# A two-layer hybrid trunk: POOL's elementwise work in the mixers and qkv moves to DVE, and half of the S5 state copies from DVE to ACT

## The chip, the cores and the metric

The kernel runs on one core of a Trainium2 chip. The metric is device time in microseconds (us), and lower is better. A core has five engines with a queue of instructions each: PE (matmul; the weight loads are listed as PEld), DVE (VectorE), ACT (ScalarE), POOL (GpSimd) and SP (SyncE, which here only starts transfers). Each works through its own queue in order, and semaphores make one engine wait for another. POOL can start transfers too.

## The reference

The model is one inference step of a two-layer trunk with D = 1024 on 1280 tokens: 1024 latent and 256 context tokens. Layer 0 feeds one input projection to two mixers. One is a bidirectional S5, a diagonal complex recurrence of 32 groups with 16 channels and 64 states each, then a GLU; the other a bidirectional gated linear attention (GLA) with 4 heads in chunks of 64 tokens. Layer 1 is grouped-query attention with rotary positions. A squared-ReLU MLP of width 4096 follows each.

```python
lam_bar = jnp.exp(lam * dt)
b_bar = ((lam_bar - 1.0) / lam)[..., None] * Bm
bu = jnp.einsum('blgc,gpc->blgp', uc, b_bar)
...
_, hs = lax.associative_scan(_lin_rec, (a, bu), reverse=rev, axis=1)
...
y = y + jnp.real(jnp.einsum('blgp,gcp->blgc', hs, Cm))
...
g = jax.nn.gelu(y.reshape(B, L, S5_WIDTH))
out = g * jax.nn.sigmoid(g @ w_glu.astype(f32) + b_glu.astype(f32))
```

A chunk of the GLA multiplies queries and keys by exponentials of a running sum of gates, and carries a state S from chunk to chunk:

```python
b = jnp.cumsum(gc, axis=1)
qd = qc * jnp.exp(b)
kd = kc * jnp.exp(-b)
...
S = S * jnp.exp(b_last)[..., None] + jnp.einsum('bshk,bshv->bhkv', kc * jnp.exp(b_last[:, None] - b), vc)
```

## The kernel before

**Numbers.** All is fp32. A matmul gets fp32 accuracy from a split: a high part `hi`, which ACT rounds by a copy, and a low part `lo = src - hi`, an elementwise subtraction. `dense` (L404 to L406) is three matmuls per 128 rows: hi·hi, lo·hi, hi·lo. Weights come by `wload`: a transfer on SP's queue, ACT's copy (L236), and the subtraction (L237), on POOL unless an engine is given, into a ring of four tiles. `split` (L384, L385) and `affine` (L391 to L393) do the same for activations. Tokens go in three blocks of 512, 512 and 256.

**Layer 0.** After the adaLN sums and the first norm come the projections of the S5 input u; then side jobs run between the matmuls of the projections of q, k, v and r. A side job is a Python generator; `dense` gives it a turn each time some modelled microseconds have passed (`tick`), and a tile scheduler with a model of the engines then sets the order of every queue.

- `s5_prep` and `s5_tables` build the tables of the S5: complex products with `cmul` (L417 to L422, six elementwise instructions) and two halves of 24 triples of products, three instructions on DVE (L652 to L654) and three on POOL (L656 to L658), sixteen times over.
- `s5_in` runs over 16 pairs of groups. For each, `cmul` makes weights, on POOL for every third pair and on DVE else; PE transposes them (L719) and multiplies (L755). For direction 0 ACT copies the states from PSUM to SBUF (L758), for direction 1 DVE does (L760); a small DVE copy per direction (L761) keeps the final states. After every four pairs `s5_join` combines neighbours: three products (L790) and six sums (L795) on DVE for each of two directions.
- `s5_chain` is 38 serial steps, each a multiply (L813) and two sums (L817, L818) on DVE. Then come eight joins, by four units and two directions; the last of them runs on POOL.
- `gla_gates` makes twelve tiles of gates: a matmul (L1000), ACT's exponentials, DVE's minimum (L1003), scan (L1009, L1011), difference (L1017) and product (L1020), and on POOL a subtraction (L1006) and two products (L1021, L1022). Results go to memory by SP's queue and come back as `wkd`.
- `s5_out` loads its tables kd, cld and ug on POOL's queue (L855, L857, L858), multiplies, and applies the GELU; `glu` projects the result. `gla_first` transposes the returned keys (L1067), multiplies (L1078) and forms 76 chunk states on DVE (L1091). `gla_second` uses them, with one product on POOL (L1196).

**Layer 1.** In qkv, `rope_tile` shuffles on DVE (L1736), multiplies on POOL (L1737) and on DVE (L1738) and sums on DVE (L1739), 20 times with 512 elements; the weights of q are subtracted on POOL. The MLPs' and the attention's own work on POOL (L1463, L1902, L1999, L2000) is another matter and stays.

Of the kernel before, what the change touches and what calls it, by code (L numbers as in the profile page):

```python
# [5 lines left out]
F32 = mybir.dt.float32  # L6
# [4 lines left out]
OP = mybir.AluOpType  # L11
# [213 lines left out]

def wload(s, src, n=1024, eng=None, own=False):

    nc = s.nc
    hi, lo = [s.A([n], F32R) for _ in range(2)] if own else (s.wr[0](), s.wr[1]())
    st = s.A.f32(lo)  # L230
    shp = list(src.shape)
    dst = st[:, :n]
    if len(shp) == 3:
        dst = dst.rearrange("p (a b) -> p a b", a=shp[1])
    nc.sync.dma_start(dst, src)
    nc.scalar.activation(hi[:, :n], st[:, :n], AF.Copy)  # L236
    (eng or nc.gpsimd).tensor_tensor(lo[:, :n], st[:, :n], hi[:, :n].bitcast(F32), OP.subtract)  # L237
    return hi, lo
# [142 lines left out]
def split(s, hi, lo, src, k=0):  # L381

    nc = s.nc
    nc.scalar.activation(hi, src, AF.Copy)  # L384
    (nc.gpsimd if k % 2 else nc.vector).tensor_tensor(lo, src, hi.bitcast(F32), OP.subtract)  # L385


def affine(s, t, a, b, hi, lo, k):

    nc = s.nc  # L390
    nc.scalar.activation(hi, t, AF.Identity, bias=b, scale=a)  # L391
    nc.vector.tensor_scalar(t, t, a, b, OP.mult, OP.add)
    (nc.vector if k % 4 == 0 else nc.gpsimd).tensor_tensor(lo, t, hi.bitcast(F32), OP.subtract)  # L393

# [137 lines left out]
def s5_prep(s):  # L532
# [62 lines left out]
    for d in range(2):  # L595
        cfb = [cf[:, i, 16 * d:16 * d + 16, None].to_broadcast([128, 16, 16]) for i in range(2)]
        cmul(nc.gpsimd, Bb[:, 0, 16 * d:16 * d + 16], Bb[:, 1, 16 * d:16 * d + 16], cfb,
             [t.B[:, 0], t.B[:, 1]], w1, w2)
# [38 lines left out]
def s5_tables(s):  # L637
# [6 lines left out]
    for st in range(8):  # L644
        un, b = divmod(st, 2)
        CL = cl()
        for d in range(2):
# [6 lines left out]
            e.tensor_tensor(CL[:, 0, d], CL[:, 0, d], tw[0], OP.subtract)  # L654
            e = nc.gpsimd
            e.tensor_tensor(CL[:, 1, d], P[0], C[2], OP.mult)  # L656
# [37 lines left out]
def s5_in(s):  # L694
# [12 lines left out]
    def weights(g2):  # L707
        wt, t1, t2 = wtr(), tr[0](), tr[1]()
        a = [pin[:, j, :, g2, :, None].to_broadcast(sh) for j in range(2)]
        b = [Bb[:, j, :, g2, None, :].to_broadcast(sh) for j in range(2)]  # L710
        cmul(nc.gpsimd if g2 % 3 == 0 else nc.vector, wt[:, 0], wt[:, 1], a, b, t1, t2)
        return wt
# [27 lines left out]
    for g2 in range(16):  # L740
# [9 lines left out]
        for d in range(2):  # L750
# [6 lines left out]
            if d == 0:  # L757
                nc.scalar.activation(H[0][:, g2, :, 1:160], pv[:, :, 0:159], AF.Copy)  # L758
            else:
                nc.vector.tensor_copy(H[1][:, g2, :, 0:159], pv[:, :, 1:160])  # L760
            nc.vector.tensor_copy(fin[:, :, d, g2], pv[:, :, 160 + d])  # L761
# [36 lines left out]
def s5_chain(s):  # L798
# [30 lines left out]
    for un in range(4):  # L829
        for d in range(2):  # L830
            e, t = (nc.gpsimd, tm2) if (un, d) == (3, 1) else (v, tmp)
            s5_join(s, e, t, un, d, 4, 2, 0, 40)
            s5_join(s, e, t, un, d, 2, 1, 0, 80)
            yield 2.0
# [144 lines left out]
def gla_gates(s):  # L979
# [7 lines left out]
    for hp in range(2):  # L987
        for tb, (t0, n, _) in enumerate(TBS):
# [7 lines left out]
            for d in range(2):  # L996
# [8 lines left out]
                nc.scalar.activation(a, a, AF.Ln, bias=1.0)  # L1005
                nc.gpsimd.tensor_tensor(mm, mm, a, OP.subtract)  # L1006
                b, r, w = a, s.rst[:, :n], mm
# [12 lines left out]
                v.scalar_tensor_tensor(e, e, 0.125, q, OP.mult, OP.mult)  # L1020
                nc.gpsimd.tensor_tensor(f, f, k, OP.mult)  # L1021
                nc.gpsimd.tensor_tensor(w, w, k, OP.mult)  # L1022
                for h in range(2):
# [77 lines left out]
def gla_second(s, hm):  # L1101
# [63 lines left out]
    def finish(u):  # L1165
# [21 lines left out]
        for h in range(2):  # L1187
# [7 lines left out]
            v.scalar_tensor_tensor(os[h][:, :n], os[h][:, :n], s.gla_norm, pb[:, :n], OP.mult, OP.mult)  # L1195
            nc.gpsimd.tensor_tensor(os[h][:, :n], os[h][:, :n], rt[:, h, :n], OP.mult)  # L1196
            split(s, *acts(hm[tb])(4 + 2 * hp + h), os[h][:, :n])
# [183 lines left out]
def mixer_half(s, l, w_src, h):  # L1381

    nc = s.nc
    wsrc = w_src.rearrange("(k p) m -> p k m", p=128)
    for j in range(4):
        w = wload(s, wsrc[:, 0:4, 256 * j:256 * j + 256], eng=nc.vector)
        for tb in range(3):
# [5 lines left out]
def mixer_out(s, l, w_src, key, part, h, ready):  # L1393
# [10 lines left out]
    if l == 0:  # L1404
        kept = [wload(s, wsrc[:, 4:8, 256 * j:256 * j + 256], eng=nc.vector, own=True) for j in range(4)]

    def weights(m):
        if l == 0:
            w = kept[m // 2]
            return lambda tb: dense(s, w, 4, lambda k: acts(h[tb])(4 + k), TBS[tb][1], off=128 * (m % 2), ms=256)  # L1410
        w = wload(s, wsrc[:, :, 128 * m:128 * m + 128], eng=nc.vector)
        return lambda tb: dense(s, w, KT, acts(h[tb]), TBS[tb][1])
# [319 lines left out]
def rope_tile(s, out, x, t0, n):  # L1732
# [3 lines left out]
    nc.vector.stream_shuffle(sw[:, :n], x, [i ^ 1 for i in range(32)])  # L1736
    nc.gpsimd.tensor_tensor(out, x, s.rope[0][:, t0:t0 + n], OP.mult)  # L1737
    nc.vector.tensor_tensor(sw[:, :n], sw[:, :n], s.rope[1][:, t0:t0 + n], OP.mult)  # L1738
# [18 lines left out]
def qkv(s, h):  # L1757
# [100 lines left out]
    for gi, grp in enumerate((tiles[0:4],) + tuple(tiles[i:i + 1] for i in range(4, 12))):  # L1858
        ws = [wload(s, wsrc[:, :, 128 * c:128 * c + 128], eng=nc.vector if gi == 0 else None) for _, _, c in grp]
        for tb in range(3):  # L1860
# [507 lines left out]
```

## Time and profile before

| | before |
|---|---|
| median of 3 runs | 3299.71 us (3296.11 to 3301.27) |
| profiled execution, its own time | 3298.78 us |
| its span, first to last instruction | 3296.4 us |
| mean granted TensorE clock, share of full speed | 0.960 |
| PE busy | 3063.6 us (93%) |
| PEld busy | 2563.4 us (78%) |
| DVE busy | 2259.9 us (69%), 4290 instructions |
| ACT busy | 1333.8 us (40%) |
| POOL busy | 726.1 us (22%), 659 instructions |

The profile is of one execution. An engine is busy while an instruction of its own runs; time in which it waits counts as idle, but an instruction that has begun and is held up within is listed with a longer duration. Over the whole span the shares say little, since layer 0's mixers make up only the first fifth; stretches say more. The groups below are single lines of such views.

### The profile page before, as it was taken

What the parts mean: (1) busy time and instruction counts of PE and PEld (TensorE: products, weight loads), DVE (VectorE), ACT (ScalarE), POOL (GpSimd) and SP (SyncE); (2) the same over time, 40 slices, a digit from 0 to 9 for tenths busy, and PEclk for the clock granted to TensorE, in tenths of its full rate; (3) what the DMA queues carried; (4) which work ended last, traced back from release to release, by engine and by line L of the source; (5) the groups of instructions that cost most, each with busy time, mean ns of one, the idle gap of its engine ahead of it and who ended that gap; (6) DMA issues with size and microseconds to landing.
All of it is one profiled execution on the core that took longest, in us unless ns stands there. A gap on an engine that the chain in (4) does not pass through costs nothing. (4 is left out here: it accounts for less than half of the span.)

```text
span 3296.4 us, 48459 instructions
## 1 busy us (share of the span) xinstructions
PE 3063.6 (93%) x17458; PEld 2563.4 (78%) x17458; DVE 2259.9 (69%) x4290; ACT 1333.8 (40%) x2485; POOL 726.1 (22%) x659
## 2 busy tenths in 40 slices
PE   7987876999999999999987999999999999999999
PEld 3665556887888887777776888888988888888787
DVE  4576993557876575767875467777488665677868
ACT  3321422423533353423332257777354333543332
POOL 3443452010000013333402212211000000244332
PEclk9998887999999999999988989999999999999999
DMA  9532668533443465656421100100435334543424
GB/s 324 145 91 84 188 204 246 186 114 104 141 138 131 138 202 192 202 166 201 134 80 50 66 31 20 33 14 16 147 122 175 133 123 138 168 141 97 134 92 155
DMA packets 402083, 433.89 MB, mean 132 GB/s; under 512 B 45708, under 2 KB 286820, under 8 KB 396212
## 3 DMA queue, kind: packets, MB, share of 16 engines
q1 hardware_dynamic: 398704, 418.66, 39.8%
q0 software_dynamic: 3136, 12.13, 1.2%
q8 instruction: 138, 2.26, 0.3%
q14 instruction: 105, 0.83, 0.1%
HBM read 296.78 MB, written 133.92 MB: 131 GB/s over the span
## 5 line engine op out<-in xcount | busy, mean ns | idle before, releaser
L1453 PE MATMUL banks<-sb_512r 128*128 128x512 f32 x5376 | 1280.3, 394 | 35.8 <-DVE sb L1649 24.0
L1453 PEld LDWEIGHTS banks<-sb_512r 128*128 128x128 f32 x5376 | 1001.5, 190 | 264.5 <-issue 29.8
L1462 ACT ACTIVATE sb_512r<-sb 128x512 fp32r<-128x512 f32 x786 | 482.8, 630 | 851.9 <-DMA sb<-in_w_mlp_out 212.8
L1463 POOL TENSOR_TENSOR sb_512r<-sb,sb_512r 128x512 fp32r<-128x512 f32 x256 | 350.6, 1396 | 1450.2 <-DMA md<-sb 949.4
L1463 DVE TENSOR_TENSOR sb_512r<-sb,sb_512r 128x512 fp32r<-128x512 f32 x530 | 400.4, 787 | 52.1 <-ACT sb_512r L1462 47.4
L1649 DVE TENSOR_TENSOR sb<-sb,banks 128x512 f32<-128x512 f32 x472 | 319.0, 683 | 158.2 <-PE banks L1453 145.5
L404 PE MATMUL banks<-sb_512r,sb_1024r 128*128 128x512 f32 x640 | 263.5, 412 | 11.0 <-ACT sb_512r L391 6.8
L405 PE MATMUL banks<-sb_512r,sb_1024r 128*128 128x512 f32 x640 | 259.6, 406 | 0.0
L406 PE MATMUL banks<-sb_512r,sb_1024r 128*128 128x512 f32 x640 | 257.9, 405 | 0.2 <-DVE sb_512r L393 0.2
L1959 DVE TENSOR_TENSOR sb_1024r<-banks,sb_1024r 128x512 fp32r<-128x512 f32 (+1 forms) x208 | 136.5, 665 | 51.3 <-ACT sb_1024r L1958 50.0
L1934 ACT ACTIVATE sb<-banks,sb,sb 128x512 f32<-128x512 f32 (+1 forms) x208 | 157.3, 765 | 20.9 <-DVE sb L1931 20.0
L1922 DVE TENSOR_REDUCE sb<-banks 128x1 f32<-128x512 f32 (+1 forms) x208 | 136.7, 664 | 33.7 <-PE banks L1921 31.6
L404 PEld LDWEIGHTS banks<-sb_512r,sb_1024r 128*128 128x128 f32 x640 | 125.4, 196 | 41.7 <-ACT sb_512r L391 7.8
L1476 PE MATMUL banks<-sb_256r,sb_512r 128*128 128x256 f32 x512 | 147.0, 287 | 6.2 <-ACT sb_512r L1462 6.2
L1477 PE MATMUL banks<-sb_256r,sb_512r 128*128 128x256 f32 x512 | 147.4, 288 | 4.9 <-DVE sb_512r L1463 4.7
L406 PEld LDWEIGHTS banks<-sb_512r,sb_1024r 128*128 128x128 f32 x640 | 124.0, 194 | 34.8 <-issue 4.4
L405 PEld LDWEIGHTS banks<-sb_512r,sb_1024r 128*128 128x128 f32 x640 | 125.4, 196 | 29.9 <-issue 6.3
L1476 PE MATMUL banks<-sb_512r 128*128 128x256 f32 x512 | 146.2, 285 | 1.1 <-DVE sb L1649 1.1
L1478 PE MATMUL banks<-sb_256r,sb_512r 128*128 128x256 f32 x512 | 146.6, 287 | 0.0
L1477 PE MATMUL banks<-sb_512r 128*128 128x256 f32 x512 | 145.4, 284 | 0.0
L1478 PE MATMUL banks<-sb_512r 128*128 128x256 f32 x512 | 145.0, 283 | 0.0
L1958 ACT ACTIVATE sb_1024r<-banks 128x512 fp32r<-128x512 f32 (+1 forms) x208 | 118.5, 583 | 62.7 <-PE banks L1955 59.6
(372 smaller groups left out, 5761.2 us busy)
## 6 DMA issues: line engine op xcount, KB each, us to landing
md<-sb SPq DMA_DIRECT2D x256, 256.0 KB
sb<-md SPq DMA_DIRECT2D x256, 256.0 KB
sb<-in_w_mlp_in SPq DMA_DIRECT2D x168, 256.0 KB
sb<-in_w_ada SPq DMA_DIRECT2D x40, 1024.0 KB
sb<-in_w_mlp_out SPq DMA_DIRECT2D x128, 256.0 KB
sb<-xd SPq DMA_DIRECT2D x72, 256.0 KB
xd<-sb SPq DMA_DIRECT2D x48, 256.0 KB
sb<-in_w_in_e SPq DMA_DIRECT2D x16, 512.0 KB
```

What stands on the lines that cost most here:

```text
L404: nc.tensor.matmul(p[:mw, :n], hi[:, a:b], xh, start=(k == 0), stop=False)
L405: nc.tensor.matmul(p[:mw, :n], lo[:, a:b], xh, start=False, stop=False)
L406: nc.tensor.matmul(p[:mw, :n], hi[:, a:b], xl, start=False, stop=(k == kt - 1))
L1453: nc.tensor.matmul(bank, x[:, o], y, start=first and k == 0 and i == 0, stop=last and k == len(B) - 1 and i == 2, skip_group_check=True)
L1462: s.nc.scalar.activation(hi, raw, AF.Copy)
L1463: e.tensor_tensor(lo, raw, hi.bitcast(F32), OP.subtract)
L1476: nc.tensor.matmul(o, hi, xh, start=(k == 0), stop=False)
L1477: nc.tensor.matmul(o, lo, xh, start=False, stop=False)
L1478: nc.tensor.matmul(o, hi, xl, start=False, stop=(k == n - 1))
L1649: v.tensor_tensor(d, d, x, OP.add)
L1922: v.tensor_reduce(m[:, kb:kb + 1], p, AX.X, OP.max)
L1934: nc.scalar.activation(P[:, 512 * i:512 * i + w], p, AF.Exp, bias=m[:, 4:5], scale=sc, accum_out=m[:, 6 + i:7 + i])
```

## The change

Every elementwise instruction that POOL had in layer 0's mixers and in layer 1's qkv goes to DVE. These are the subtractions of weights and activations in `wload`, `split` and `affine`, the complex products of `s5_prep` and of every third pair in `s5_in`, half of the products of `s5_tables`, the last join, three instructions of each gate tile, one of `gla_second` and one of `rope_tile`. In the other direction the state copy of direction 1 in `s5_in` goes from DVE to ACT. The joins behind the chain take their scratch tile by direction. Nothing is added or left out; `mixer_half` and `mixer_out` gave `wload` DVE already and lose only the argument. POOL's queue falls from 635 rows to 417. Line numbers behind line 655 are one lower in the changed kernel.

```diff
-def wload(s, src, n=1024, eng=None, own=False):
+def wload(s, src, n=1024, own=False):
...
     nc.scalar.activation(hi[:, :n], st[:, :n], AF.Copy)
-    (eng or nc.gpsimd).tensor_tensor(lo[:, :n], st[:, :n], hi[:, :n].bitcast(F32), OP.subtract)
+    nc.vector.tensor_tensor(lo[:, :n], st[:, :n], hi[:, :n].bitcast(F32), OP.subtract)
...
-    (nc.gpsimd if k % 2 else nc.vector).tensor_tensor(lo, src, hi.bitcast(F32), OP.subtract)
+    nc.vector.tensor_tensor(lo, src, hi.bitcast(F32), OP.subtract)
...
-    (nc.vector if k % 4 == 0 else nc.gpsimd).tensor_tensor(lo, t, hi.bitcast(F32), OP.subtract)
+    nc.vector.tensor_tensor(lo, t, hi.bitcast(F32), OP.subtract)
...
-        cmul(nc.gpsimd, Bb[:, 0, 16 * d:16 * d + 16], Bb[:, 1, 16 * d:16 * d + 16], cfb,
+        cmul(v, Bb[:, 0, 16 * d:16 * d + 16], Bb[:, 1, 16 * d:16 * d + 16], cfb,
...
             e.tensor_tensor(CL[:, 0, d], CL[:, 0, d], tw[0], OP.subtract)
-            e = nc.gpsimd
             e.tensor_tensor(CL[:, 1, d], P[0], C[2], OP.mult)
...
-        cmul(nc.gpsimd if g2 % 3 == 0 else nc.vector, wt[:, 0], wt[:, 1], a, b, t1, t2)
+        cmul(nc.vector, wt[:, 0], wt[:, 1], a, b, t1, t2)
...
             else:
-                nc.vector.tensor_copy(H[1][:, g2, :, 0:159], pv[:, :, 1:160])
+                nc.scalar.activation(H[1][:, g2, :, 0:159], pv[:, :, 1:160], AF.Copy)
...
-            e, t = (nc.gpsimd, tm2) if (un, d) == (3, 1) else (v, tmp)
+            e, t = (v, (tmp, tm2)[d])
...
-                nc.gpsimd.tensor_tensor(mm, mm, a, OP.subtract)
+                nc.vector.tensor_tensor(mm, mm, a, OP.subtract)
...
-                nc.gpsimd.tensor_tensor(f, f, k, OP.mult)
-                nc.gpsimd.tensor_tensor(w, w, k, OP.mult)
+                nc.vector.tensor_tensor(f, f, k, OP.mult)
+                nc.vector.tensor_tensor(w, w, k, OP.mult)
...
-            nc.gpsimd.tensor_tensor(os[h][:, :n], os[h][:, :n], rt[:, h, :n], OP.mult)
+            nc.vector.tensor_tensor(os[h][:, :n], os[h][:, :n], rt[:, h, :n], OP.mult)
...
-    nc.gpsimd.tensor_tensor(out, x, s.rope[0][:, t0:t0 + n], OP.mult)
+    nc.vector.tensor_tensor(out, x, s.rope[0][:, t0:t0 + n], OP.mult)
...
-        ws = [wload(s, wsrc[:, :, 128 * c:128 * c + 128], eng=nc.vector if gi == 0 else None) for _, _, c in grp]
+        ws = [wload(s, wsrc[:, :, 128 * c:128 * c + 128]) for _, _, c in grp]
```

The scheduler places the moved instructions anew. On DVE, in the chain of `s5_chain`, the queue held single instructions of half-size gate tiles between the steps. `sb_128_115` and `sb_128_2017` are the chain's two scratch tiles, `sb_10240_87` its states, and `sb_512_...` gate tiles. Before:

```order
L813 TENSOR_TENSOR sb_128_115<-sb_10240_87,sb_128_808 128x128
L1003 TENSOR_SCALAR sb_512_2065<-banks,sb_48_272 128x256
L817 TENSOR_TENSOR sb_10240_87<-sb_10240_87,sb_128_115 128x2x2x16
L818 TENSOR_TENSOR sb_10240_87<-sb_10240_87,sb_128_115 128x2x2x16
L813 TENSOR_TENSOR sb_128_2017<-sb_10240_87,sb_128_808 128x128
L1009 SCALAR_TENSOR_TENSOR sb_512_2063<-sb_512_2056,sb_512_2065 128x256
L817 TENSOR_TENSOR sb_10240_87<-sb_10240_87,sb_128_2017 128x2x2x16
L1017 TENSOR_TENSOR sb_512_2065<-sb_512_2063 128x256
L818 TENSOR_TENSOR sb_10240_87<-sb_10240_87,sb_128_2017 128x2x2x16
```

The changed kernel has there (L812, L816, L817 are the chain):

```order
L1005 TENSOR_TENSOR sb_512_2065<-sb_512_2065,sb_512_2063 128x512
L812 TENSOR_TENSOR sb_128_2017<-sb_10240_87,sb_128_808 128x128
L1005 TENSOR_TENSOR sb_512_2066<-sb_512_2066,sb_512_2064 128x512
L1008 SCALAR_TENSOR_TENSOR sb_512_2063<-sb_512_2056,sb_512_2065 128x512
L816 TENSOR_TENSOR sb_10240_87<-sb_10240_87,sb_128_2017 128x2x2x16
L1010 SCALAR_TENSOR_TENSOR sb_512_2064<-sb_512_2056,sb_512_2066 128x512
L1016 TENSOR_TENSOR sb_512_2065<-sb_512_2063 128x512
L817 TENSOR_TENSOR sb_10240_87<-sb_10240_87,sb_128_2017 128x2x2x16
L1016 TENSOR_TENSOR sb_512_2066<-sb_512_2064 128x512
L1019 SCALAR_TENSOR_TENSOR sb_512_2067<-sb_512_2067,sb_1024_2062 128x512
L1020 TENSOR_TENSOR sb_512_2069<-sb_512_2069,sb_1024_2062 128x512
```

Two gate tiles, with POOL's former subtraction (L1005) and product (L1020), now stand between the steps; all twelve tiles fall into the chain's stretch.

On POOL, at the end of the joins, stood the last join (`sb_640_2585` is its scratch), two weight subtractions and then the loads of `s5_out`:

```order
L795 TENSOR_TENSOR sb_10240_87<-sb_10240_87,sb_640_2585 128x2x4x40
L237 TENSOR_TENSOR sb_1024r<-sb_1024_278,sb_1024r 128x1024
L795 TENSOR_TENSOR sb_10240_87<-sb_10240_87,sb_640_2585 128x2x4x40
L237 TENSOR_TENSOR sb_1024r<-sb_1024_320,sb_1024r 128x1024
L858 DMA sb_1280_3970<-ug 128x1280
L858 DMA sb_1280_3971<-ug 128x1280
L858 DMA sb_1280_3969<-ug 128x1280
L855 DMA sb_1024_3967<-kd 16x8x128 x4
```

Now the same loads follow memsets:

```order
L973 MEMSET sb_512_2056 128x8
L726 MEMSET sb_1296_957 128x8x2
L726 MEMSET sb_1296_958 128x8x2
L968 MEMSET sb_512_796 32x512
L857 DMA sb_1280_3970<-ug 128x1280
L857 DMA sb_1280_3971<-ug 128x1280
L857 DMA sb_1280_3969<-ug 128x1280
L854 DMA sb_1024_3967<-kd 16x8x128 x4
```

No instruction of arithmetic is left ahead of the loads.

On DVE, where the joins end, GLA states (L1091, into `sb_1024_...`) stood between the instructions of the joins:

```order
L790 TENSOR_TENSOR sb_640_2584<-sb_10240_87,sb_128_807 128x640
L1091 SCALAR_TENSOR_TENSOR sb_1024_3474<-sb_1024_3474,sb_40_2059,banks 128x128
L795 TENSOR_TENSOR sb_10240_87<-sb_10240_87,sb_640_2584 128x2x4x40
L1091 SCALAR_TENSOR_TENSOR sb_1024_3474<-sb_1024_3474,sb_40_2059,banks 128x128
L795 TENSOR_TENSOR sb_10240_87<-sb_10240_87,sb_640_2584 128x2x4x40
L1091 SCALAR_TENSOR_TENSOR sb_1024_3474<-sb_1024_3474,sb_40_2059,banks 128x128
L790 TENSOR_TENSOR sb_640_2584<-sb_10240_87,sb_128_806 128x640
```

Now the joins of both directions alternate to their end and the states follow in rows (L1090):

```order
L789 TENSOR_TENSOR sb_640_2584<-sb_10240_87,sb_128_806 128x640
L789 TENSOR_TENSOR sb_640_2585<-sb_10240_87,sb_128_806 128x640
L794 TENSOR_TENSOR sb_10240_87<-sb_10240_87,sb_640_2584 128x2x4x40
L794 TENSOR_TENSOR sb_10240_87<-sb_10240_87,sb_640_2585 128x2x4x40
L794 TENSOR_TENSOR sb_10240_87<-sb_10240_87,sb_640_2584 128x2x4x40
L794 TENSOR_TENSOR sb_10240_87<-sb_10240_87,sb_640_2585 128x2x4x40
L1059 MEMSET sb_1024_3476 128x128
L863 COPY sb_10240_87<-sb_10240_87 64x4x160 x2
L1090 SCALAR_TENSOR_TENSOR sb_1024_3474<-sb_1024_3474,sb_40_2059,banks 128x128 x7
```

All 76 states stand behind the last join.

## Rows read from the trace of the kernel before

**Rows 1.** Stretches: length, busy PE, PEld, DVE, ACT, POOL; clock, DMA share, GB/s.

```profile
0.00:161.30 161.30, 129.54 (x682) 86.03 (x682) 86.78 (x266) 59.75 (x91) 63.65 (x70) 0.94 0.75 238
161.30:327.90 166.60, 129.11 (x1040) 104.15 (x1038) 114.83 (x238) 32.53 (x71) 71.29 (x77) 0.90 0.30 87
327.90:496.40 168.50, 136.97 (x701) 92.32 (x701) 159.75 (x252) 62.01 (x128) 84.59 (x67) 0.85 0.66 195
496.40:575.30 78.90, 53.62 (x457) 47.75 (x457) 25.58 (x73) 19.49 (x35) 16.51 (x29) 0.73 0.81 244
575.30:640.00 64.70, 61.60 (x370) 52.83 (x371) 39.38 (x80) 30.32 (x53) 3.97 (x4) 0.92 0.50 157
1725.00:1825.00 100.00, 83.20 (x446) 70.98 (x445) 54.72 (x150) 31.25 (x57) 27.14 (x15) 0.86 0.16 48
```

**Rows 2.** Timeline of POOL, 409 to 498 us: start, duration, instruction.

```profile
409.82 2.34 POOL L237 TENSOR_TENSOR sb_1024r<-sb,sb_1024r 128x1024 fp32r<-128x1024 f32 x1
...
493.83 4.16 POOL L855 DMA_DIRECT2D sb<-kd  x8 [1.27 <-DMA sb<-kd]
```

**Rows 3.** Timeline of DVE, 407 to 498 us, same columns.

```profile
407.63 0.26 DVE L818 TENSOR_TENSOR sb<-sb,sb 128x64 f32<-128x64 f32 x1
...
410.02 2.27 DVE L818 TENSOR_TENSOR sb<-sb,sb 128x64 f32<-128x64 f32 x1
412.32 0.38 DVE L813 TENSOR_TENSOR sb<-sb,sb 128x128 f32<-128x128 f32 x1
...
495.81 1.02 DVE L795 TENSOR_TENSOR sb<-sb,sb 128x320 f32<-128x320 f32 x2
```

**Rows 4.** DVE by line, 100 to 500 us: count, busy, mean ns, idle before.

```profile
L795 DVE TENSOR_TENSOR sb<-sb,sb 128x320 f32<-128x320 f32 (+1 forms) x90 | 68.4, 760 | 1.3
L790 DVE TENSOR_TENSOR sb<-sb,sb 128x640 f32<-128x640 f32 (+1 forms) x45 | 57.4, 1275 | 0.6
L813 DVE TENSOR_TENSOR sb<-sb,sb 128x128 f32<-128x128 f32 x38 | 20.4, 536 | 1.0
L817 DVE TENSOR_TENSOR sb<-sb,sb 128x64 f32<-128x64 f32 x38 | 20.0, 527 | 0.9
L818 DVE TENSOR_TENSOR sb<-sb,sb 128x64 f32<-128x64 f32 x38 | 17.1, 451 | 0.9
...
L760 DVE COPY sb<-banks 128x318 f32<-128x318 f32 x16 | 7.7, 482 | 6.3 <-PE banks L755 6.3
```

**Rows 5.** DVE by line, 460.5 to 480 us.

```profile
L795 DVE TENSOR_TENSOR sb<-sb,sb 128x320 f32<-128x320 f32 x16 | 9.8, 614 | 0.3
L790 DVE TENSOR_TENSOR sb<-sb,sb 128x640 f32<-128x640 f32 x8 | 8.2, 1021 | 0.2
```

**Rows 6.** DVE by line, 1660 to 1960 us.

```profile
L1739 DVE TENSOR_TENSOR sb<-sb,sb 128x512 f32<-128x512 f32 x20 | 21.0, 1051 | 2.3 <-POOL sb L1737 1.2
...
L393 DVE TENSOR_TENSOR sb_512r<-sb,sb_512r 128x512 fp32r<-128x512 f32 x16 | 10.8, 688 | 0.0
...
L237 DVE TENSOR_TENSOR sb_1024r<-sb,sb_1024r 128x1024 fp32r<-128x1024 f32 x2 | 2.4, 1222 | 0.0
```

**Rows 7.** POOL by line, 0 to 620 us.

```profile
L237 POOL TENSOR_TENSOR sb_1024r<-sb,sb_1024r 128x1024 fp32r<-128x1024 f32 x18 | 44.5, 2476 | 63.4 <-ACT sb_1024r L236 44.3 <-PE banks L406 19.1
...
L1021 POOL TENSOR_TENSOR sb<-sb,sb 128x512 f32<-128x512 f32 (+1 forms) x12 | 16.6, 1380 | 24.1 <-ACT sb L1016 24.1
```

**Rows 8.** Waits of PE, 0 to 620 us: total, times, longest.

```profile
PE banks L1067 <- DMA sb<-wkd: 12.0, 2, 6.1
PE banks L1078 <- DVE sb L1091: 11.5, 6, 4.7
```

**Rows 9.** Waits of DVE, 161.3 to 327.9 us, same columns.

```profile
DVE sb L761 <- ACT sb L758: 17.1, 5, 11.3
DVE sb L417 <- POOL sb L422: 8.0, 3, 4.9
```

**Rows 10.** Line 1091 on DVE: shortest, median, longest ns, first and last start.

```profile
L1091 DVE SCALAR_TENSOR_TENSOR sb<-sb,sb,banks x76: 326/348/364, 471.3 to 569.6; 128x128 f32<-128x128 f32 x76
```

More of the change, by code (lines that the diff above doesn't have):

```diff
@@ L1381, in mixer_half @@
 def mixer_half(s, l, w_src, h):
-    nc = s.nc
     wsrc = w_src.rearrange("(k p) m -> p k m", p=128)
     for j in range(4):
-        w = wload(s, wsrc[:, 0:4, 256 * j:256 * j + 256], eng=nc.vector)
+        w = wload(s, wsrc[:, 0:4, 256 * j:256 * j + 256])
         for tb in range(3):
@@ L1404, in mixer_out @@
     if l == 0:
-        kept = [wload(s, wsrc[:, 4:8, 256 * j:256 * j + 256], eng=nc.vector, own=True) for j in range(4)]
+        kept = [wload(s, wsrc[:, 4:8, 256 * j:256 * j + 256], own=True) for j in range(4)]
     def weights(m):
@@ L1410, in weights @@
             return lambda tb: dense(s, w, 4, lambda k: acts(h[tb])(4 + k), TBS[tb][1], off=128 * (m % 2), ms=256)
-        w = wload(s, wsrc[:, :, 128 * m:128 * m + 128], eng=nc.vector)
+        w = wload(s, wsrc[:, :, 128 * m:128 * m + 128])
         return lambda tb: dense(s, w, KT, acts(h[tb]), TBS[tb][1])
```

## The prediction

> **What bounds the kernel now.** The first view to read is the table of stretches [rows 1]. I cut the span at four places of layer 0 and call the pieces A (0 to 161.3 us: weights, norm, preparation), B (161.3 to 327.9: the S5 input), C (327.9 to 496.4: the S5 chain and its joins, the gates), D (496.4 to 575.3: S5 output, GLA states) and F (1725 to 1825, qkv of layer 1). Behind D, PE is busy 61.6 of 64.7 us and stays so to the end but for F, so only gaps of PE in these pieces are to be had: 31.8 us in A, 37.5 in B, 31.5 in C, 25.3 in D, 16.8 in F. In C the reader is to see DVE busy 159.75 of 168.5 us: C is DVE's stretch. In B and D DVE has room, and the waits decide.
>
> The second view is the timeline of POOL and DVE side by side [rows 2, 3]. A sum of the S5 chain, 64 elements, takes 0.26 us on DVE at 407.63, where POOL stands, but 2.27 us at 410.02, where POOL subtracts 1024 elements from 409.82 to 412.16; the chain's multiply right after takes 0.38. So a DVE instruction with two operands in SBUF stands still while POOL works. The third view groups DVE's instructions by line and says how often: the chain's multiply has a mean of 536 ns, its two sums 527 and 451 [rows 4], far above 0.38 and 0.26. The joins show it too: 760 ns for a sum and 1275 for a product on the mean [rows 4], 614 and 1021 in a stretch in which POOL is idle [rows 5]. So POOL's work is not free cover beside DVE; DVE pays for most of it in standing time.
>
> **Price of a moved instruction.** The 1024-wide subtraction costs 1.222 us on DVE [rows 6] against 2.476 on POOL [rows 7], a 512-wide instruction 0.688 [rows 6] against a gate product's 1.380 [rows 7]. About half, so I enter POOL's busy time at one half.
>
> **A: 0.** DVE takes 32 us (half of 63.65) into 74 us of idle time. The DMA engines are busy 0.75 of A [rows 1] with weights and x, which no part of the change touches, so I allow a gain of at most a third of PE's 31.8 us of gaps, 10; a loss of at most three weight subtractions ahead of the norm on DVE's queue, 3 × 1.222 = 3.7. I take 0, nearest to what the DMA share says.
>
> **B: −8.** DVE's account: 114.83, + 71.29 / 2 = 35.6 moved in, − 16 × 0.482 = 7.7 of state copies moved out [rows 4], − the standing time, 48 × 0.146 + 24 × 0.254 = 13.1 for the first joins (three products and six sums for each of eight): 129.6 of 166.6 us. It still has room. The wait of DVE for POOL's products, 8.0 us [rows 9], is gone; I take that. Against it: the small copies of final states wait 17.1 us for ACT's state copy of the same bank [rows 9], and once both directions are copied by ACT twice as many may do so. ACT has the time for the copies themselves, being busy 32.5 of 166.6. Ends: −20 (the 8.0, and a third of PE's 37.5 us of gaps), +17 (the wait for ACT doubles).
>
> **C: −4.** Standing time on DVE: 38 × (0.536 − 0.38) + 38 × (0.527 − 0.26) + 38 × (0.451 − 0.26) = 23.3 for the chain [rows 3, 4]; the 42 sums and 21 products of the seven joins on DVE give 42 × 0.146 + 21 × 0.254 = 11.4: 35 in all. Twenty GLA states at 0.348 [rows 10] go behind the joins, as the order of the program shows: −7. POOL's 84.6 us less some 8.5 of DMA issues, halved, come in: +38. So 159.75 − 35 − 7 + 38 = 155.8, and with the 8.8 us idle of now 164.6 for 168.5: −4. The moved work pays for itself just about; the saving is thin. Ends: −20 (idle time goes as well, and less of the gates falls between chain steps), +15. The bad end: DVE works in order, and the gates' products now stand between the chain's steps. If the exponential from ACT is late there, the chain stands; POOL waited 24.1 us for it and 63.4 for weights [rows 7], off to one side.
>
> **D: −8.** Two things wait here: PE for the GLA weights' way through memory, 12.0 us, and for the states, 11.5 [rows 8]. POOL issued the loads of S5's output behind the last join and two subtractions, of which one waited 19.1 us for PE [rows 7]; now they stand right behind its memsets and may start when their buffers and tables are there, so the DMA engines, 0.81 busy in D [rows 1], begin earlier. Against that, all 76 states stand behind the last join: 20 more at 0.348 = 7 us if they come in a row, but 20 × 73 / 56 = 26 at the pace of the 56 that came between 496.8 and 569.6 [rows 3, 10]. Ends −25 (all of PE's gaps in D), +15; I take two thirds of the 12.0 us.
>
> Here a rule speaks against the change. The row: eight loads issued from POOL took 4.16 us, 0.52 each [rows 2], from 493.83 on, while DVE ran joins with two operands in SBUF to 496.83 [rows 3]. The Trainium skill ("SBUF — State Buffer", "SBUF: two separate sides") says that DVE in a two-port mode keeps GpSimd from writing the descriptors of its own DMAs, and gives about 620 ns alone against 3100 beside such an operation. By that, 40 loads (32 of kd, 4 of cld, 4 of ug) beside the joins would cost an estimated 40 × 2.5 = 100 us of POOL's queue; the trace doesn't agree for these joins. I enter 0, and leave it 0.02 of the slower case.
>
> **F: −4.** Twenty rope sums take 1.051 us [rows 6] beside POOL's rope products and weights; a subtraction of the same size shows 0.688 alone: −7.3. The products moved in cost 20 × 0.688 = 13.8, in 45 us of DVE idle, and the tile's chain (shuffle, two products, sum) hardly shortens. PE's gaps there are 16.8 us. Ends −14 and +3.
>
> **Sum.** 0 − 8 − 4 − 8 − 4 = −24 on the profiled execution's 3298.78 us: 3274.8. The median of the three runs is 0.9 above that execution, so I forecast **3276 us**. The granted clock was 0.85 in C and 0.73 in D against 0.92 behind them [rows 1]; with fewer gaps it may rise, which I don't count.
>
> **Rivals.** *The gaps close further.* If the late end of C is what holds D's loads, B and D go to their low ends and C to three quarters of its own: −20 − 15 − 25 = −60, 3240 us. For it: the share of DMA in D; against it: 11.5 us of waits for states have nothing to do with POOL.
>
> *No change.* DVE only exchanges standing time for work: in A to C +32 + 36 + 38 = 106 comes in, and 35 + 13 + 8 = 56 of standing time and copies go out, so it ends with 50 us more to do, and what PE waited for by way of POOL it now waits for by way of DVE. 3300 us. The Trainium skill ("Perfetto Trace Analysis", "Optimizing Scalar/DVE Operations") says that moving work between GpSimd and DVE may not help, since they share a port; by that rule this is the case. The standing rows agree with the port, and C's account, 164.6 against 168.5, speaks for a small gain only, and what stands for more is the waits.
>
> *Slower.* One queue takes over the other's waits: POOL waited 63.4 us for weights (44.3 for ACT's copy, 19.1 for PE to free the bank) and 24.1 for the exponentials [rows 7], 87.5 in sum. DVE inherits them in order, ahead of chain and joins. It decides when over 24 us come through, the size of my gains; at half, 44: 3298.8 − 24 + 44 = 3319 us, 3320 as a median. Against it: the scheduler puts chain steps between, and POOL's waits began early because it had nothing else to do.
>
> **How the numbers follow.** Forecast (3255 to 3292) 0.55; gaps close further 0.13; no change 0.14; slower 0.18. The bound of 0.2% is 6.6 us, about what a measurement of this kernel can tell from no change. So faster 0.68, same 0.14, slower 0.18. The range is 3236 to 3308: it takes in the forecast with the bounds of its terms, the closing of the gaps and no change, and leaves out the worse half of the slower case and a little below.
>
> **What would show it.** The chain's multiply near 0.38 us and its sums near 0.26 on the mean, join sums near 0.614, with POOL idle in A to C; the last join before 490 us instead of 496.8, and the GLU's first product, now at the end of D, near 555. Wrong, if DVE shows a wait of over 10 us for ACT or PE at a gate product or a weight subtraction in C; if the small state copies wait over 30 us for ACT in B; or if DVE's chain is fast and the GLU starts no earlier, because the states or their loads come late.

## The result: 0.3 to 0.5% slower, and the profile after

The changed kernel took 3315.32 us in the median of 10 runs, the kernel before 3299.66; the ratio is 1.0052, with a 95% interval of 1.0036 to 1.0067. A second set of runs gave 1.0033 (1.0017 to 1.0048). So it is 11 to 17 us slower; forecast were 24 us faster, and the range ended at 3308. Below, "the change" is this kernel, with a profiled span of 3314.7 us.

The table of stretches is cut at the events of [rows 1]: first state copy, first chain step, end of the joins, first GLU product (first start of lines 757 and 812, end of line 794, start of L404 on `sb_2048r`), and the same 100 us of qkv, 6 us later. Columns as in [rows 1].

```profile
0.00:152.00 152.00, 126.55 (x656) 82.13 (x658) 94.82 (x319) 58.41 (x89) 5.21 (x16) 0.92 0.78 249
152.00:330.80 178.80, 149.88 (x1204) 122.60 (x1200) 117.39 (x301) 42.65 (x98) 0.74 (x3) 0.90 0.30 89
330.80:491.80 161.00, 110.19 (x481) 70.58 (x478) 134.63 (x284) 60.63 (x121) 15.44 (x29) 0.79 0.71 213
491.80:567.60 75.80, 55.95 (x498) 48.39 (x498) 24.63 (x75) 17.94 (x36) 8.45 (x14) 0.74 0.69 208
1731.00:1831.00 100.00, 79.01 (x403) 66.88 (x403) 53.92 (x157) 29.83 (x54) 0.00 (x0) 0.83 0.15 44
```

By these events the pieces before were 160.8, 167.1, 168.9 and 78.5 us. A is 8.8 us shorter, C (161.0) 7.9 and D (75.8) 2.7, but B is 178.8 where it was 167.1. DVE's lines between 100 and 500 us, to be read against [rows 4]:

```profile
L794 DVE TENSOR_TENSOR sb<-sb,sb 128x320 f32<-128x320 f32 (+1 forms) x96 | 51.4, 564 | 0.6
L789 DVE TENSOR_TENSOR sb<-sb,sb 128x640 f32<-128x640 f32 (+1 forms) x48 | 45.7, 973 | 0.2
L237 DVE TENSOR_TENSOR sb_1024r<-sb,sb_1024r 128x1024 fp32r<-128x1024 f32 x15 | 18.3, 1220 | 33.1 <-ACT sb_1024r L236 33.1
L812 DVE TENSOR_TENSOR sb<-sb,sb 128x128 f32<-128x128 f32 x38 | 14.6, 384 | 0.6
L816 DVE TENSOR_TENSOR sb<-sb,sb 128x64 f32<-128x64 f32 x38 | 10.2, 269 | 0.6
L817 DVE TENSOR_TENSOR sb<-sb,sb 128x64 f32<-128x64 f32 x38 | 10.2, 268 | 0.6
L653 DVE TENSOR_TENSOR sb<-sb,sb 128x288 f32<-128x288 f32 x16 | 7.2, 450 | 15.5 <-DMA cld<-sb 15.5
L655 DVE TENSOR_TENSOR sb<-sb,sb 128x288 f32<-128x288 f32 x16 | 7.1, 451 | 16.5 <-DMA cld<-sb 16.5
```

The standing time beside POOL is gone: the chain's three lines went from 536, 527 and 451 ns to 384, 269 and 268, the joins from 760 and 1275 to 564 and 973. The new numbers stand behind the second bar: DVE waited 33.1 us at weight subtractions, for ACT's copy of arriving weights, and 32.0 us at table products, for the last table to be written to memory. All of the second and over half of the first fall into B. Waits of DVE there, 152 to 330.8 us (total, times, longest):

```profile
DVE sb_1024r L237 <- ACT sb_1024r L236: 18.2, 4, 11.0
DVE sb L655 <- DMA cld<-sb: 16.5, 4, 5.6
DVE sb L653 <- DMA cld<-sb: 15.5, 3, 6.2
```

Before, between 161.3 and 327.9 us, DVE had of these only the wait at its own half of the table products; the other two stood on POOL, beside it:

```profile
DVE sb L653 <- DMA cld<-sb: 17.7, 3, 10.0
POOL sb L656 <- DMA cld<-sb: 35.2, 4, 16.9
POOL sb_1024r L237 <- ACT sb_1024r L236: 17.9, 3, 10.5
```

Behind the chain PE has a hole. First PE's longest wait between 432 and 500 us, then rows of ACT's timeline (start, duration, instruction, idle time before and its releaser):

```profile
PE banks L1077 <- ACT sb L1068: 38.1, 1, 38.1
```

```profile
479.12 1.36 ACT L862 ACTIVATE sb<-sb 64x640 f32<-64x640 f32 x2 [7.11 <-DVE sb L794]
...
491.53 0.73 ACT L862 ACTIVATE sb<-sb 64x640 f32<-64x640 f32 x1 [7.11 <-DVE sb L794]
492.17 1.05 ACT L1068 ACTIVATE sb<-banks 128x512 f32<-128x512 f32 x2
```

PE has run out of projections at 440 us and of all other matmuls at 454.7; its next work is the GLA states, whose keys (L1068) stand on ACT's queue behind S5's state swaps (L862), which wait for the joins.

In qkv each rope instruction is down to 0.69 us, as forecast, and DVE waits 16.0 us for arriving weights (1660 to 1960 us).

```profile
L1737 DVE TENSOR_TENSOR sb<-sb,sb 128x512 f32<-128x512 f32 x20 | 13.7, 687 | 0.2
L1735 DVE TENSOR_TENSOR sb<-sb,sb 128x512 f32<-128x512 f32 x20 | 13.7, 683 | 9.1 <-ACT sb L1841 9.1
L237 DVE TENSOR_TENSOR sb_1024r<-sb,sb_1024r 128x1024 fp32r<-128x1024 f32 x10 | 12.2, 1224 | 16.0 <-ACT sb_1024r L236 16.0
```

### The profile page after: what moved, and what is told of

Same layout as the page of the kernel before. It is cut to its first block, busy times and chain, and to the rows that moved or that the text cites. A ratio compares the mean times of both kernels' runs of the same rounds, so it can differ in the third digit from the quotient of the medians.

```text
span 3314.7 us, 48375 instructions
## 1 busy us (share of the span) xinstructions
PE 3066.0 (92%) x17458; PEld 2563.1 (77%) x17458; DVE 2256.3 (68%) x4492; ACT 1339.4 (40%) x2501; POOL 460.7 (14%) x441
## 5 line engine op out<-in xcount | busy, mean ns | idle before, releaser
L404 PE MATMUL banks<-sb_512r,sb_1024r 128*128 128x512 f32 x640 | 261.0, 408 | 10.7 <-ACT sb_512r L391 6.4
L404 PEld LDWEIGHTS banks<-sb_512r,sb_1024r 128*128 128x128 f32 x640 | 123.7, 193 | 40.3 <-ACT sb_512r L391 7.4
```

Source lines behind the costliest of these rows:

```text
L404: nc.tensor.matmul(p[:mw, :n], hi[:, a:b], xh, start=(k == 0), stop=False)
```

## The experiments

The theory after the result: layer 0 is bound by the S5 path on DVE (state copies, tables, chain, joins, then S5's output), and what costs are those moved instructions that wait for memory or for arriving weights, since DVE works in order and the S5 path stands behind them. The rivals: DVE has too much work; the order of joins and GLA states makes the hole; qkv alone.

The table collects one profile of each run, in us: first state copy, from there to the chain, the chain, the joins, from the joins to the GLU (lines 758, 813, 818, 795 and L404 of the kernel before, or the same lines of each), and qkv, from the 8800th to the 9800th matmul in order of start. The last column is the ratio of times to the kernel before in the same rounds, with its interval.

| run | copy | to chain | chain | joins | to GLU | GLU | qkv | ratio |
|---|---|---|---|---|---|---|---|---|
| before | 160.8 | 167.1 | 90.0 | 78.9 | 78.5 | 575.3 | 199.6 | |
| the change | 152.0 | 178.8 | 100.8 | 60.3 | 75.8 | 567.6 | 208.8 | 1.0052 (1.0036 to 1.0067) |
| e9, again | 149.4 | 178.4 | 104.3 | 58.0 | 77.2 | 567.3 | 207.8 | 1.0033 (1.0017 to 1.0048) |
| e1 | 150.6 | 178.9 | 103.5 | 55.8 | 77.5 | 566.3 | 199.4 | 1.0021 (1.0007 to 1.0035) |
| e2 | 157.1 | 169.4 | 90.2 | 78.8 | 78.5 | 574.0 | 201.9 | 1.0006 (0.9995 to 1.0017) |
| e3 | 150.8 | 178.8 | 100.0 | 72.2 | 59.2 | 561.0 | 205.5 | 1.0026 (1.0011 to 1.0040) |
| e4 | 150.9 | 178.9 | 103.5 | 74.0 | 60.0 | 567.3 | 201.4 | 1.0003 (0.9992 to 1.0014) |
| e5 | 153.6 | 168.9 | 102.9 | 52.3 | 77.1 | 554.7 | 207.7 | 1.0016 (1.0004 to 1.0027) |
| e6 | 141.6 | 188.9 | 104.8 | 51.9 | 74.8 | 561.9 | 205.3 | 1.0012 (1.0000 to 1.0023) |
| e7 | 151.9 | 178.8 | 100.3 | 56.5 | 76.6 | 564.2 | 202.3 | 1.0040 (1.0024 to 1.0055) |
| e8 | 151.0 | 178.8 | 95.8 | 64.9 | 78.2 | 568.8 | 202.3 | 1.0060 (1.0045 to 1.0075) |
| e10 | 141.6 | 166.4 | 103.5 | 55.0 | 75.1 | 541.6 | 201.0 | 0.9955 (0.9936 to 0.9974) |
| e11 | 142.1 | 165.0 | 105.1 | 66.3 | 55.6 | 534.0 | 198.0 | 0.9881 (0.9861 to 0.9901) |
| e12 | 145.6 | 187.4 | 98.0 | 78.1 | 57.4 | 566.3 | 204.9 | 1.0022 (1.0006 to 1.0038) |
| e13 | 142.6 | 189.7 | 101.4 | 62.6 | 58.7 | 555.0 | 198.1 | 0.9977 (0.9966 to 0.9987) |
| e14 | 156.1 | 168.2 | 104.3 | 63.8 | 58.9 | 551.3 | 199.1 | 0.9992 (0.9979 to 1.0004) |
| e15 | 141.3 | 166.8 | 103.9 | 66.2 | 55.1 | 533.4 | 207.9 | 0.9911 (0.9898 to 0.9924) |
| e16 | 143.8 | 166.1 | 90.6 | 81.8 | 76.4 | 558.7 | 199.6 | 0.9956 (0.9942 to 0.9971) |

### qkv: e1 and e2

e1 is the change with these two lines undone, e2 the kernel before with only them:

```diff
-    nc.vector.tensor_tensor(out, x, s.rope[0][:, t0:t0 + n], OP.mult)
+    nc.gpsimd.tensor_tensor(out, x, s.rope[0][:, t0:t0 + n], OP.mult)
...
-        ws = [wload(s, wsrc[:, :, 128 * c:128 * c + 128]) for _, _, c in grp]
+        ws = [wload(s, wsrc[:, :, 128 * c:128 * c + 128], eng=nc.vector if gi == 0 else nc.gpsimd) for _, _, c in grp]
```

> The change with qkv of layer 1 as before: rope product and the q weights' subtractions on POOL. Theory (DVE, working in order, takes over waits that POOL had off to one side, and in qkv this costs what the two traces show, some 10 us between 1720 and 1880): the time falls by 8 to 12 us against the change, to about 3305, +6 against before. Rival 1 (all the loss comes from layer 0, and the 10 us in qkv are only a later meeting of the same work): under 3 us off the change. Rival 2 (DVE is simply too full in qkv): excluded if DVE stays under 70% busy there in the change, as its profile shows (96 of 190 us).

> The kernel before with only the qkv part of the change. Theory: +8 to +12 us, about 3309. If the blocked time of DVE beside POOL were what counts in qkv, as the prediction had it: -4 us. Rival 1: within 3 us of before.

Against the ratio of the result, 1.0052, e1 is 0.31 points under the change (10 us), as the theory has it; against that of the second set, 1.0033, it is 4 us, and the intervals overlap. e2 missed, at +2 us where 8 to 12 were expected: the number of rival 1. Its qkv took 2.3 us longer, the change's 9.2. One profile isn't enough for a difference of this size; all runs together settle below (e15) whether qkv costs anything.

### The order of joins and states: e3 and e4

```diff
-            e, t = (v, (tmp, tm2)[d])
+            e, t = (v, tmp)
```

e4 also takes qkv back. With two scratch tiles the joins of both directions run in turn to their end; with one, fifteen of the GLA states stand among them.

> The change with one scratch tile for all joins behind the chain instead of one for each direction; everything is still on DVE. In the program's order GLA states then stand among the joins again and ACT's key copies stand ahead of its state swaps. Theory (the order, not the work, makes PE's one wait of 38 us, matmul L1077 for ACT's key copy): the wait falls under 10 us and the time by 15 to 30 us against the change, to 3285 to 3300. Rival (DVE has too much work, so PE would wait for the joins in any order): PE still idle over 40 us between 430 and 500, the time within 5 us of the change.

> Both edits: one scratch tile, and qkv as before. Theory: the gains add, -25 to -40 us against the change, 3275 to 3290, faster than before by 10 to 25. If the layer 0 part has nothing to give, 3300 to 3306.

e3 gained 9 us on the change (2 against the second set) where 15 to 30 were expected, and e4 (1.0003) was no faster than before, where 10 to 25 us were expected. e4 is 8 us faster than e3, from which it differs by qkv alone. The hole was not closed, it moved. In e3 PE's longest waits between 432 and 570 us are:

```profile
PE banks L1077 <- DVE sb L1090: 42.3, 6, 36.7
PE banks L1066 <- DMA sb<-wkd: 9.6, 3, 7.1
```

PE hardly waits for ACT's key copies any more, but now it waited 36.7 us for a state behind later joins. So the rival's mechanism holds here: PE is busy 17.2 of the 70 us from 430 to 500 and waits for DVE's joins in either order. Its bound of 5 us on the time is met against the second set only. From the joins to the GLU it is 59 us instead of 76, so the order is worth something, but the joins end 10 us later, at 502.

### One group back at a time: e5 to e8

Each is the change with one group undone. e5, the tables:

```diff
             e.tensor_tensor(CL[:, 0, d], CL[:, 0, d], tw[0], OP.subtract)
+            e = nc.gpsimd
             e.tensor_tensor(CL[:, 1, d], P[0], C[2], OP.mult)
```

e6, the weights of layer 0 (`mixer_half`, `mixer_out` and qkv keep DVE by an argument):

```diff
-    nc.vector.tensor_tensor(lo[:, :n], st[:, :n], hi[:, :n].bitcast(F32), OP.subtract)
+    (eng or nc.gpsimd).tensor_tensor(lo[:, :n], st[:, :n], hi[:, :n].bitcast(F32), OP.subtract)
```

e7, the copies of direction 1, and e8, the gates:

```diff
-                nc.scalar.activation(H[1][:, g2, :, 0:159], pv[:, :, 1:160], AF.Copy)
+                nc.vector.tensor_copy(H[1][:, g2, :, 0:159], pv[:, :, 1:160])
```

```diff
-                nc.vector.tensor_tensor(mm, mm, a, OP.subtract)
+                nc.gpsimd.tensor_tensor(mm, mm, a, OP.subtract)
...
-                nc.vector.tensor_tensor(f, f, k, OP.mult)
-                nc.vector.tensor_tensor(w, w, k, OP.mult)
+                nc.gpsimd.tensor_tensor(f, f, k, OP.mult)
+                nc.gpsimd.tensor_tensor(w, w, k, OP.mult)
```

> The change with the second half of the table products (three of six per tile) back on POOL. Theory (the S5 path on DVE bounds layer 0, and DVE now waits on it for what POOL used to wait for: the table tile to be written out): from the first state copy to the first chain step 178.8 us in the change, about 167 here, as before the change (167.1); the time 5 to 12 us under the change, about 3306. Rival (the time for which DVE stands beside POOL outweighs the waits): the stretch stays over 175 us, the time within 4 us of the change or above it.

> The change with the weight subtractions of layer 0 back on POOL; qkv stays on DVE. Theory: DVE no longer waits for ACT's weight copies (34 us of such waits between 0 and 495 us in the change), the chain's stretch falls from 100.7 to about 93 us, the time 3 to 10 us under the change. Rival (standing time): the means of the chain's sums rise from 0.27 over 0.35 us, the stretch stays over 98 us, the time within 4 us of the change.

> The change with the state copies of direction 1 back on DVE, 16 of 0.48 us. Theory: no part of the loss; within 4 us of the change, the stretch from first copy to first chain step within 4 us of 178.8. Rival (both copies on ACT delay the small copies that DVE waits for): 5 to 10 us faster than the change.

> The change with the three POOL instructions of each gate tile back on POOL. Theory (occupancy of the S5 path): the chain's stretch falls from 100.7 to about 90 us, the joins' grows from 60.3 to about 70 since some stand beside POOL, the time 0 to 6 us under the change. Rival (the gates' waits for ACT on DVE are the loss): 8 to 15 us under the change.

e5 is 12 us under the change (6 against the second set) and its stretch to the chain 168.9 us: the theory's numbers. e6 gained 13 us (7), but not where it was expected: its chain took 104.8 us, not 93. What moved is the first copy, 10 us earlier, and the chain still began at 330, with 188.9 us from the copy to the chain while the tables were on DVE. e7 is within 4 us. e8 gained nothing, where 0 to 6 us were expected: the chain shortened by 5 and the joins grew by 5. The gains of e1, e3, e5 and e6 add up to 44 us by the one ratio of the change and to 19 by the other, where 17 and 11 were lost, so they are too uncertain to measure the groups by.

### Three groups at once: e9 to e12

e9 repeats the change. e10 takes the tables, layer 0's weights and qkv back to POOL together, by the edits of e5, e6 and e1; e11 adds that of e3, one scratch tile. e12 is the kernel before with these three groups on DVE:

```diff
-    (eng or nc.gpsimd).tensor_tensor(lo[:, :n], st[:, :n], hi[:, :n].bitcast(F32), OP.subtract)
+    (eng or nc.vector).tensor_tensor(lo[:, :n], st[:, :n], hi[:, :n].bitcast(F32), OP.subtract)
...
-            e = nc.gpsimd
...
-    nc.gpsimd.tensor_tensor(out, x, s.rope[0][:, t0:t0 + n], OP.mult)
+    nc.vector.tensor_tensor(out, x, s.rope[0][:, t0:t0 + n], OP.mult)
```

> The change itself once more, on the chip and in the rounds of the next three, with a second profile. 3312 to 3320, ratio to before 1.004 to 1.006. From the profile: if the second one loses 6 to 12 us between 1700 and 1910 us against before as the first did (9 us), that loss belongs to the code; if it loses under 4, part of it was that one execution's.

> The change with three groups back on POOL: half of the tables, the weight subtractions of layer 0, and qkv. Left of the change on DVE: activations' low parts, the S5 weights, the last join, gates, the product of gla_second; the copies stay on ACT, the scratch by direction. Theory (what costs is the instructions for which DVE waits in its own order, on memory or on ACT's copies of arriving weights): 3290 to 3302, no slower than before. Rival (joins, scratch and gates on DVE cost as well): 3304 to 3312.

> The same three groups back on POOL, and one scratch tile for the joins. Theory: the GLA states stand among the joins, another 5 to 10 us off, 3283 to 3297, perhaps faster than before. Rival (PE waits for the end of the joins in any order): within 4 us of the run with the scratch by direction.

> The kernel before with only these three groups moved to DVE. Theory: they bring the loss by themselves, +10 to +20 us, 3309 to 3319; first copy to first chain step over 173 us (167.1 before). Rival (only the sum of all moves fills DVE): within 5 us of before.

e9 came out at 1.0033, a little under the 1.004 to 1.006 expected, and its qkv, 207.8 us, confirms the loss there. e10 is 0.45% faster than before (15 us), and **e11 1.2%: 3262.04 us in the median, by the ratio 39 us under the kernel before**, and so faster than both. What is left of the change without the three groups is a gain, with one scratch tile a larger one than I forecast. e12 is slower than before, but by 7 us, under the 10 expected. Its chain began at 333.0, yet that is not where its loss lies: its GLU starts 9 us earlier than before, as it is 57.4 us from the joins to there and not 78.5, and its 4000th matmul comes at 751.3 us, before at 751.6. By the end of qkv it is 7 us behind. e11's stretches, cut at the same events:

```profile
0.00:142.10 142.10, 115.00 (x623) 75.47 (x625) 93.20 (x296) 57.45 (x88) 22.17 (x22) 0.96 0.82 261
142.10:307.10 165.00, 132.00 (x1030) 104.98 (x1027) 121.39 (x256) 37.85 (x88) 51.30 (x53) 0.91 0.30 90
307.10:478.40 171.30, 140.95 (x777) 101.51 (x776) 151.11 (x301) 69.19 (x138) 34.61 (x40) 0.84 0.74 224
478.40:534.00 55.60, 48.12 (x434) 42.91 (x434) 19.93 (x61) 14.51 (x29) 8.97 (x15) 0.81 0.83 252
```

A and B together end 20.8 us before those of the kernel before, and D is 23 us shorter. POOL has its waits back, off to one side of DVE's queue: its own between 100 and 331 us in e11 are

```profile
POOL sb_1024r L237 <- ACT sb_1024r L236: 94.5, 7, 62.4
POOL sb L656 <- DMA cld<-sb: 39.0, 3, 16.0
```

while DVE waits 15.1 us for tables in the same stretch, and for no weights at all.

### Each group put back into the fast kernel: e13 to e16

> The run with three groups back on POOL and one scratch tile, and from it only the tables' second half moved to DVE again. Theory (DVE waits in its order for the table tile to be written out): first copy to first chain step from 165 to over 173 us, the time 6 to 14 us above that run's 3262. Rival (the tables cost only together with the weights): within 4 us of it.

> From the same run only the weight subtractions of layer 0 moved to DVE again. Theory (DVE waits for ACT's copies of arriving weights): the first state copy later, from 142 to about 150 us, the time 6 to 14 us above 3262. Rival: within 4 us.

> From the same run only qkv moved to DVE again. Nine profiles with qkv on DVE lose 2 to 9 us against before between 1709 and 1909 us, 5.6 on the mean, four without it 0.3 on the mean: the time 3 to 9 us above 3262. Rival (qkv costs only after layer 0 of the change): within 2 us.

> From the same run the three instructions of each gate tile back on POOL. If DVE's standing beside POOL is what the move of the gates saves: chain and joins together longer by 5 us or more (171.3 us in that run), the time 3 to 15 us above 3262. If the gates on DVE only lengthen the chain: 3 to 10 us below it.

Each is e11 with one of the edits above undone: e13 without that of e5, e14 without e6's, e15 without e1's; e16 adds e8's. Against e11's ratio, which was taken in other rounds (the intervals are 0.1 to 0.2 points to either side), the tables cost 0.96 points (32 us), the weights 1.11 (37), qkv 0.30 (10), and the gates on POOL 0.75 (25). The first two are over twice the upper end of what was expected. DVE's waits from 100 to 331 us in e13 and then in e14 name the cause:

```profile
DVE sb L655 <- DMA cld<-sb: 18.2, 4, 5.6
DVE sb L760 <- ACT sb L759: 16.2, 4, 14.6
DVE sb L653 <- DMA cld<-sb: 13.0, 3, 5.1
DVE sb L760 <- ACT sb L757: 12.0, 4, 10.5
```

```profile
DVE sb_1024r L237 <- ACT sb_1024r L236: 27.7, 7, 8.3
DVE sb L653 <- DMA cld<-sb: 15.6, 3, 8.9
```

The chain begins at 332.3 us in e13 and at 324.3 in e14, against 307.1 in e11. In e13 the stretch to the chain grew by 24.7 us; DVE's waits at table products are 31.2 us (15.1 in e11) and those for ACT's state copies 28.2 (15.6), 28.7 more together; in e14 the first copy came 14.0 us later and 27.7 us of waits for weights are new. The rival that DVE merely has too much work can be read off the stretches, in e13 from copy to chain and in e14 the two pieces up to the chain:

```profile
142.60:332.30 189.70, 148.68 (x1138) 121.59 (x1135) 124.73 (x307) 41.17 (x94) 16.15 (x11) 0.88 0.29 85
```

```profile
0.00:156.10 156.10, 123.91 (x647) 81.68 (x649) 96.08 (x314) 58.55 (x90) 11.09 (x23) 0.91 0.77 244
156.10:324.30 168.20, 130.61 (x1054) 105.98 (x1050) 111.06 (x253) 38.19 (x88) 36.14 (x44) 0.91 0.31 88
```

DVE is busy 124.7 us in e13's stretch, 121.4 in e11's: 21.4 of the 24.7 us are idle time. Up to the chain it is busy 207.1 us in e14 and 214.6 in e11, so there all 17.2 us and more are idle time. Either alone brings the chain most of the way back to the 330 of the change, which is why they don't add there: e3, which is e11 with all three groups on DVE, is 48 us above it, and the three one by one make 78. In these two runs the GLU starts later as the chain does: 555.0 and 551.3 against 534.0. Part of the rest lies behind that: from there to the 4000th matmul it is 191.4 and 195.2 us, in e11 184.2.

That qkv on DVE costs time is now settled: it took 205.4 us on the mean of ten profiles (201.9 to 208.8), on POOL 199.5 on the mean of eight, the kernel before among them (198.0 to 201.4). The two groups do not overlap, and e15's 10 us, just over the 3 to 9 expected, agree with the 8 between e3 and e4. By what mechanism it costs is open: in e2 DVE waits as long for weights (19.1 us from 1660 to 1960) as in the change (16.0) and in e15 (17.3), and its qkv took 201.9 us, not 208.

e16's expectation missed in its reason and in its size, 25 us for 3 to 15. Chain and joins take 172.4 us together, against 171.3 in e11: what the chain gains by shedding the gates, the joins lose. The 25 us come behind the joins, 76.4 us to the GLU instead of 55.6. The loads of S5's tables, in e11 and then in e16, show one part of it:

```profile
L855 POOL DMA_DIRECT2D sb<-kd x32: 528/528/743, 451.9 to 504.9; - x32
```

```profile
L855 POOL DMA_DIRECT2D sb<-kd x32: 531/531/668, 476.9 to 529.1; - x32
```

They begin 25 us later. How much of the loss is theirs, and how much the later keys', was not separated.

## Why the prediction was wrong

- **Price and standing time: right.** The moved instructions cost what the rows said (1.220 us for 1.222, 0.69 for 0.688), and the chain lines fell to 384, 269 and 268 ns where 0.38 and 0.26 us stood.
- **C, −4: the right way, by a sum that is not right.** 161.0 us against 168.9, so −7.9 for −4. The gates lengthened the chain by 11 us, and the joins, unblocked, gave back 19. DVE was busy 134.6 us where I had added up 155.8, and idle 26.4 where I kept 8.8: it waited 9.1 us for weights, 6.1 for S5's state swaps and 7.7 for ACT at gate tiles. Two errors of some 20 us met, so that the size came out near is in part luck. The twenty GLA states that I took out of C were fifteen; the other five stood behind the joins.
- **A, 0:** −8.8, within its bound of 10. But the bound was too narrow: with layer 0's weights on POOL (e6, e10) A takes 141.6 us, 19 less than before, and the weights' waits on DVE take ten of that back.
- **B, −8: the step that failed.** It came out at +11.7. I added up DVE's work (129.6 of 166.6 us), found room, and took over only the wait that vanished, 8.0 us. POOL's waits in the same stretch, 35.2 us for the table tile and 17.9 for weights, stood in its view of waits and are put at nothing: the moved instructions wait in DVE's order, ahead of the chain. DVE's work was even less than I had it, 117.4 us, but it stood idle for 61.4, with 32.0 us of waits for tables (17.7 before) and 18.2 for weights (none before). e5 and e13 show it for the tables and e14 for the weights. The end of B that I gave, +17 by ACT's copies, lay near the outcome from a wrong cause: those waits fell from 17.1 to 8.9 us (e7 moves nothing).
- **D, −8, and "behind D PE is busy to the end":** D gave −2.7. The loads did start early, at 431 us, but PE waited 38.1 us for keys, in C. Nor was it busy behind the GLU's start: 56.68 of 70 us from 570 to 640, 64.78 before. From the GLU's start to the 4000th matmul the change took 12.6 us longer (188.9 against 176.3), a term that was missing in my sum.
- **F, −4: wrong in sign.** The −4 itself was not worked out: my rows gave −7.3 and +13.8 for DVE. The rope sums became as short as forecast, and the stretch grew by 9.2 us in this profile (PE busy 3.9 us more, idle 5.3 more), 5.9 on the mean. My bounds of −14 and +3 left out that DVE would wait 16.0 us for weights with the rope tiles behind them. That this wait is what PE then meets is not shown, and e2, with the same wait and little loss, speaks against it. The cause in qkv stays open.
- **The sum:** −8.8 + 11.7 − 7.9 − 2.7 + 12.6 + 9.2 = +14.1 of the 18.3 us between the two spans; of the last 4 us, 1.4 lie between the 4000th and the 8800th matmul and 2.7 behind qkv. So layer 0, forecast at −20, lost 4.9 us up to the 4000th matmul, with large terms that offset each other, and qkv lost more.
- **The rivals.** The slower one named the mechanism, one queue taking over the other's waits, its place at the weights, and 3320 us; it happened with the weights (33.1 us of waits on DVE, of 63.4 on POOL, over the bound of 24) and with the tables, which it did not name. The gates' exponentials, its other half, let nothing through to the moved products: a product that DVE had already stands ahead of them and waits 4.2 us, 4.6 before. It had 0.18, too little: its price and its row both stood in the text, and I set it aside because the scheduler would put chain steps between; DVE still stood up to 11.0 us at one weight.
- **The signs.** None of the three signs of being wrong came up clearly: waits in C of 9.1 us at weights and 4.2 at a gate product, each under the bound of 10, 8.9 at the small state copies for 30, and the GLU 7.7 us earlier, though at 567.6 and not near 555. They looked for the loss in C and at the copies, and it stood in B and in qkv.
- **The rules of the Trainium skill.** The first, that POOL and DVE share a port and that moving work between them might not help: the Trainium skill ("Perfetto Trace Analysis", "Optimizing Scalar/DVE Operations"). The standing time agrees with the port (527 ns beside POOL, 269 without). e11 and the change move work between the same two engines with −39 and +11 to +17 us, so here what the moved instructions wait for decided. The other, on POOL's own DMAs, has no case here: the Trainium skill ("SBUF — State Buffer", "SBUF: two separate sides") speaks of DVE in a two-port mode, and by its part "Who interferes with whom" a `tensor_tensor`, which is what the joins are, has none. So the 100 us that I worked out by it never stood against the change. The trace agrees: in the change S5's loads were issued beside the joins, and a row of POOL's timeline there reads

```profile
430.56 3.73 POOL L854 DMA_DIRECT2D sb<-kd  x7 [0.93 <-PE banks L406]
```

which is 0.53 us each, for 0.52 before.

## What to carry to other kernels

Before moving an instruction to a busier engine, read what it waits for where it stands, and not only what it costs: a wait that is free on an idle queue can stand in front of everything behind it on the new one. Here the change without three groups gained 15 us, and 39 with the states among the joins; the three groups, two of them with such waits and the third, qkv, for a reason still open, turned it into a loss of 11 to 17. Not every wait comes along: the gate products had waited 24.1 us on POOL and waited for nothing on DVE, where an instruction ahead of them met the wait. Undo groups together and then put them back one at a time, and don't expect the costs to add: 78 us one by one were 48 together.

## What the runs showed that I had not expected

- A second scratch tile, which removes a false dependence between the joins, cost 24 us in e10 against e11: with both directions ready at once, the scheduler ran the joins to their end and all GLA states behind them. The joins end sooner (55.0 us for 66.3), but the GLU starts 7.6 us later and the 4000th matmul comes 16.4 us later. With the gates on DVE it is 74.8 to 77.5 us from the joins to the GLU in the seven runs with two tiles, and 55.1 to 60.0 in the six with one.
- The granted clock was 0.53 of full speed, close to the lower of its two levels (1.2 and 2.4 GHz), in the change between 431.6 and 491.8 us, where PE was busy 9.4 us of 60, and 0.74 in the stretch behind it, when PE worked again.
